# One hybrid decoder layer in fp32: the engines' queues ordered by the detailed timeline model instead of the simple one

## The chip, the cores and the metric

The kernel runs on one core of a Trainium2 chip. The metric is the device time of one launch in microseconds (us). The engines named here are PE (TensorE, matmuls; PEld is its weight load), DVE (VectorE), ACT (ScalarE), POOL (GpSimd) and SP (SyncE, which issues the DMAs). Each engine works through its own queue strictly in order, and waits at the head of it on semaphores that other engines or DMAs raise. [...]

## The reference

One decoder layer on 256 tokens of width 2048, batch 1, depth 1, all in fp32. A conditioning vector c gives shifts, scales and gates for both halves. Eight heads are stick-breaking attention, eight are sparse attention (DSA) over the 64 best keys of an indexer.

```
mod = silu(c) @ w_ada + b_ada
sh1, sc1, g1, sh2, sc2, g2 = split(mod, 6)
h = rmsnorm(x, norm1_g) * (1 + sc1) + sh1
q_sb, k_sb, v_sb, q_ds, k_ds, v_ds, q_ix, k_ix, w_ix = split(h @ w_in)
# stick-breaking: w[t,s] = exp(log_sigmoid(z[t,s]) + sum over s<j<t of log_sigmoid(-z[t,j])), s < t
o_sb = stick_breaking_attention(q_sb, k_sb, v_sb)       # z = q k^T / sqrt(128)
o_ds = dsa_attention(q_ds, k_ds, v_ds, q_ix, k_ix, w_ix) # top 64 keys of a score, softmax, p @ v
merged = concat(rmsnorm(o_sb, sb_norm_g), rmsnorm(o_ds, dsa_norm_g))
x = x + g1 * (merged @ w_out)
h2 = rmsnorm(x, norm2_g) * (1 + sc2) + sh2
u = causal_conv3(h2 @ w_up) ; gate, val = split(u)       # 2 x 5504 columns
x = x + g2 * ((silu(gate) * val) @ w_down)
return rmsnorm(x, final_norm_g)
```

## The kernel before

Everything lies transposed in the on-chip memory: features on the 128 partitions, tokens along the free axis. Each fp32 weight piece of 1 MB is loaded by SP, and each half of it is split into a high part (a cast on ACT, L145, names ending in h) and a low part (a subtraction on DVE, L146, names ending in l). A product is then three matmuls per 128 x 128 block: high by high, low by high and high by low (L173 to L175 in `trn`, which gives the transposed result). The raw pieces have 4 buffers, and so have the high and the low parts.

The stages in program order: the norm of x and the adaLN vector; the columns of `w_in` for the indexer and the DSA heads; the DSA heads with their norm (sums of squares rdsp, broadcast rdsb, reciprocal root rdsy at L126, normalised od split into odh and odl); the values V; then for each stick-breaking head h the projection QK(h) (chunks QK10 to QK17 in the names) and `sb_head(h)`; then the output projection O in groups of column blocks, the first half of it on the DSA heads (O<-odh, odl), the second half on the stick-breaking heads (O<-osh, osl), which needs their norm (rsbp, rsbv, rsby, rsbb); then the FFN with its up (U) and down (W) products.

A stick-breaking head goes back and forth between three engines:

```
z = pt[:, 0:384]                                   # L671-673: three matmuls on PE
A.copy(out=zs, in_=z)                              # L675
A.activation(e, z, AF.Abs)                         # L677, then Exp L678 and Ln L679
V.scalar_tensor_tensor(out=e, in0=z, scalar=0.0, in1=e, op0=ALU.max, op1=ALU.add)   # L680
T.matmul(pt[:, 0:384], lhsT=negu, rhs=e, start=True, stop=False)                    # u, L682-683
V.tensor_tensor(out=w, in0=pt[:, 0:384], in1=zs, op=ALU.add)                        # L685
A.activation(w, w, AF.Exp)                                                          # L686
T.matmul(po[:, 0:S], lhsT=vsb[:, 0, h * P:(h + 1) * P], rhs=w[:, 0:S], ...)         # o, L688-689
A.activation(os_[:, h, :], po[:, 0:S], AF.Copy, ...)                                # L690
A.activation(sq, po[:, 0:S], AF.Square)                                             # L695
V.tensor_tensor(out=sqs, in0=sqs, in1=sq, op=ALU.add)                               # L696
```

z, u and o, the DSA matmuls and the broadcasts of the norms share four PSUM banks (tag att), which are handed out in program order; QK, V and O share the other four (tag acc). So z of head 0 cannot stand ahead of rdsb in PE's queue.

Between the stages `pump()` issues pieces of the adaLN product for the later shifts and gates: most as a multiplication with a running sum on DVE (wa, L225), five groups as matmuls on PE (ap, L202, 4 loads wg of 4 matmuls each, transposed by aq, L210).

The program does not fix the order between independent instructions. When the context that L964 opens is closed, a scheduling pass plays the whole program through on a model of the engines, and at each step puts next into an engine's queue the earliest instruction in program order that is ready by the model's time. What stands in the queues is then fixed; on the chip each engine keeps to it.

## Time and profile before

| | |
|---|---|
| three runs | 1221.39 us median (1220.79 to 1223.54) |
| profiled execution | 1222.48 us, span 1220.7 us from the first to the last instruction |
| mean granted clock of TensorE | 0.976 |
| busy | PE 1154.4 us (95%), DVE 879.5 (72%), ACT 632.2 (52%) |
| DMA | 303.48 MB, mean 249 GB/s |
| the chain that ended last | PE 89%, DVE 6%, ACT 3%, DMA 1% |

The engine with the largest share is PE. The chain that ended last is followed back from the last instruction, at each step to what released it; PE's 89% of it says that for most of the span the next matmul waited only for the one before it.

### The profile page before, as it was taken

To read this page: it belongs to the slowest core of one execution; us is meant where nothing else is said; L and a number is where in the kernel's file an instruction comes from. 1 tells how busy PE (TensorE), PEld (TensorE's weight loads), DVE (VectorE), ACT (ScalarE), POOL (GpSimd) and SP (SyncE) were. 2 spreads that over 40 slices of the span, in tenths; PEclk is the share of its full clock that TensorE was granted. 3 is DMA by queue.
4 is the path that set the end of the run, shared out by engine and by line. 5 is a ranking of instruction groups with operands and counts; after the bars stand their busy time and mean duration, and the time that the engine had idled before them with its cause. 6 is when DMAs were issued, how large, how long until landed. Compare 5 with 4: busy or idle time off the path is not lost.

```text
span 1220.7 us, 17725 instructions
## 1 busy us (share of the span) xinstructions
PE 1154.4 (95%) x7120; PEld 1018.6 (83%) x7120; DVE 879.5 (72%) x1267; ACT 632.2 (52%) x1004; POOL 0.2 (0%) x4
## 2 busy tenths in 40 slices
PE   3699999899999797999999999999999999999996
PEld 2578997668878797999888888888888888888885
DVE  4877787689766698878789787787876745454543
ACT  3356554457465344456565556555655644444441
POOL 0000000000000000000000000000000000000000
PEclk9799999899999898999999999999999999999998
DMA  8988899668788498776568666675665555555541
GB/s 308 391 318 333 330 324 335 256 222 329 260 341 331 141 346 306 246 275 238 177 246 336 241 210 225 222 254 208 246 224 202 178 198 183 196 184 189 191 139 69
DMA packets 43282, 303.48 MB, mean 249 GB/s; under 512 B 4928, under 2 KB 5440, under 8 KB 7232
## 3 DMA queue, kind: packets, MB, share of 16 engines
q1 hardware_dynamic: 43200, 302.35, 68.1%
q8 instruction: 55, 0.90, 0.3%
q14 instruction: 27, 0.22, 0.0%
HBM read 300.24 MB, written 2.10 MB: 248 GB/s over the span
## 4 chain that ended last, share of the span: by engine, by line
PE 89%; DVE 6%; ACT 3%; DMA 1%; issue 1%; SPq 0%; DVEq 0%; ACTq 0%
PE U L168 21%; PE W L168 13%; PE U L166 11%; PE W L166 7%; PE U L173 3%; PE U L174 3%; PE U L175 3%; PE O L174 3%; PE O L175 3%; PE QK L173 3%; PE QK L175 3%; PE O L173 3%; PE QK L174 3%; DVE wa L225 2%; PE ap L202 1%; PE A L151 1%
## 5 line engine op out<-in xcount | busy, mean ns | idle before, releaser
L225 DVE SCALAR_TENSOR_TENSOR wa<-wa,scb 128x2048 f32<-128x2048 f32 x76 | 173.2, 2284 | 3.8 <-DMA wa<-wa 3.5
L844 ACT COPY u<-U 128x256 f32<-128x256 f32 x70 | 26.1, 372 | 116.6 <-PE U L168 116.6
L845 DVE TENSOR_TENSOR u<-U,u 128x256 f32<-128x256 f32 x70 | 29.3, 420 | 58.7 <-ACT u L844 58.7
L855 DVE SCALAR_TENSOR_TENSOR uc<-u,par,uc 128x255 f32<-128x255 f32 (+1 forms) x140 | 63.8, 478 | 0.8
L851 ACT ACTIVATE uc<-u,par 128x256 f32<-128x256 f32 x70 | 41.9, 601 | 0.0
L862 ACT CAST aT<-uc 128x256 fp32r<-128x256 f32 x43 | 17.4, 404 | 33.3 <-DVE uc L861 33.3
L323 ACT ACTIVATE amul<-mod,b,par 128x1 f32<-128x1 f32 x32 | 12.1, 385 | 42.8 <-DVE wa L225 42.6
L890 DVE SCALAR_TENSOR_TENSOR x1T<-W,mod,x1T 128x256 f32<-128x256 f32 x16 | 7.7, 481 | 31.1 <-PE W L166 31.1
L741 ACT ACTIVATE x2q<-x1T 128x256 f32<-128x256 f32 x15 | 6.3, 418 | 39.1 <-DVE x1T L736 39.0
L326 ACT ACTIVATE mod<-mod,par 128x1 f32<-128x1 f32 x32 | 8.5, 294 | 30.5 <-DVE wa L225 29.4
L202 PE MATMUL ap<-wg,csil 128*32 128x512 f32 x160 | 23.5, 642 | 0.7 <-DMA wg<-wg 0.5
L857 ACT ACTIVATE uc<-uc 128x256 f32<-128x256 f32 x43 | 17.9, 416 | 7.7 <-DVE uc L855 7.6
L861 DVE TENSOR_TENSOR uc<-uc 128x256 f32<-128x256 f32 x43 | 18.2, 422 | 2.8
L863 DVE TENSOR_TENSOR aT<-uc,aT 128x256 fp32r<-128x256 f32 x43 | 18.0, 418 | 0.8 <-ACT aT L862 0.7
L855 DVE SCALAR_TENSOR_TENSOR uc<-U,par,uc 128x255 f32<-128x255 f32 (+1 forms) x32 | 15.0, 478 | 1.0 <-ACT uc L851 0.6
L686 ACT ACTIVATE sbt<-sbt 128x384 f32<-128x384 f32 x8 | 4.2, 525 | 20.6 <-DVE sbt L685 20.6
L202 PEld LDWEIGHTS ap<-wg,csil 128*32 128x32 f32 x160 | 4.3, 115 | 9.4 <-issue 7.0
L736 DVE SCALAR_TENSOR_TENSOR x1T<-O,mod,xT 128x256 f32<-128x256 f32 x16 | 7.0, 479 | 6.7 <-PE O L175 6.7
L555 PE MATMUL rel<-ws,qixT 64*128 64x128 f32 (+1 forms) x64 | 9.8, 390 | 1.5 <-ACT rl L560 1.5
L207 ACT COPY rw<-ap 128x512 f32<-128x512 f32 x5 | 2.9, 581 | 15.5 <-PE ap L202 15.5
L283 PE MATMUL cb<-ident,csil 128*128 128x128 f32 x16 | 3.6, 423 | 7.6 <-DMA ident<-ident 7.6
L151 PE MATMUL A<-wA00h,hh 128*128 128x512 f32 x4 | 2.5, 669 | 8.5 <-ACT hh L318 8.5
(2810 smaller groups left out, 4042.8 us busy)
## 6 DMA issues: line engine op xcount, KB each, us to landing
wU<-wU SPq DMA_DIRECT2D x86, 1024.0 KB, 4.8
wa<-wa SPq DMA_DIRECT2D x76, 1024.0 KB, 6.3
wD<-wD SPq DMA_DIRECT2D x43, 1024.0 KB, 4.8
wg<-wg SPq DMA_DIRECT2D x20, 1024.0 KB, 7.1
wA<-wA SPq DMA_DIRECT2D x16, 1024.0 KB, 6.7
wQK<-wQK SPq DMA_DIRECT2D x16, 1024.0 KB, 6.1
wO<-wO SPq DMA_DIRECT2D x16, 1024.0 KB, 5.7
xT<-xT SPq DMA_DIRECT2D x4, 512.0 KB, 6.0
```

Source lines behind the costliest of these rows:

```text
L166: T.matmul(pt[:, 1, :], lhsT=wl, rhs=x[:, 0, :], start=False, stop=stop)
L168: T.matmul(pt, lhsT=wh, rhs=x, start=first, stop=stop)
L173: T.matmul(pt, lhsT=wh, rhs=xh, start=first, stop=False)
L174: T.matmul(pt, lhsT=wh, rhs=xl, start=False, stop=False)
L175: T.matmul(pt, lhsT=wl, rhs=xh, start=False, stop=last)
L202: T.matmul(pt[32 * j:32 * j + 32, :], lhsT=csil[:, k:k + 1].to_broadcast([P, 32]), rhs=w[:, j * 512:(j + 1) * 512], start=q == 0, stop=q == 3)
L225: i = V.scalar_tensor_tensor(out=w, in0=w, scalar=1.0, in1=scb, op0=ALU.mult, op1=ALU.mult, accum_out=mod[:, j:j + 1])
L844: A.copy(out=u[:, gv, :], in_=acc[gv][:, 1, :])
L845: V.tensor_tensor(out=u[:, gv, :], in0=acc[gv][:, 0, :], in1=u[:, gv, :], op=ALU.add)
L851: A.activation(uc[:, gv, :], u[:, gv, :], AF.Identity, scale=par[:, PCW + 3 * i + 2:PCW + 3 * i + 3], bias=par[:, PCB + i:PCB + i + 1])
L855: V.scalar_tensor_tensor(out=uc[:, gv, sft:S], in0=u[:, gv, 0:S - sft], scalar=par[:, o:o + 1], in1=uc[:, gv, sft:S], op0=ALU.mult, op1=AL ...
L861: V.tensor_tensor(out=uc[:, 1, :], in0=uc[:, 0, :], in1=uc[:, 1, :], op=ALU.mult)
```

## The change

The context is opened with the detailed timeline model for its scheduling pass:

```diff
-    with tile.TileContext(nc) as tc:
+    with tile.TileContext(nc, schedule_with_timeline_sim=True) as tc:
         layer(tc, aps, out)
```

No instruction is added or removed. PE's list of 4226 rows differs from the one before in 1418 lines; DVE's and ACT's differ with it. In SP's queue only three loads near the masks at the start change places, and POOL's is the same.

On PE, where the first stick-breaking head begins (z_2529 is its z), the order before is as follows; QK_2554 and QK_2647 are the projections QK11 and QK12, and rdsb is the broadcast of the DSA norm.

```order
L175 MATMUL QK_2554<-hh_1352,wQK1110l 128x256
L173 MATMUL QK_2647<-hh_1352,wQK1200h 128x256
L174 MATMUL QK_2647<-hl_1353,wQK1200h 128x256
L129 MATMUL rdsb<-ident,rdsy 128x128 x2
L671 LDWEIGHTS identb
L671 MATMUL z_2529<-sbm,identb 128x384
L672 MATMUL z_2529<-qk_198 128x256
L673 MATMUL z_2529<-qk_198 128x128
L175 MATMUL QK_2647<-hh_1352,wQK1200l 128x256
L173 MATMUL QK_2647<-hh_1352,wQK1200h 128x256
```

Behind it follow 284 more matmuls of QK12 to QK17, mixed with u0, o0, z1 and the next heads. After the change the same z stands here, with the last DSA steps (av, pp), the last adaLN product (ap_3184) and the sum rdsp in front of it, and a matmul of the first O block behind it:

```order
L637 MATMUL av_2248<-pT_2171,ws 128x512
L202 MATMUL ap_3184<-wg_3197,csil 32x512 x4
L637 MATMUL av_2256<-pT_2171,ws 128x512 x2
L202 MATMUL ap_3184<-wg_3266,csil 32x512 x4
L115 MATMUL rdsp<-nones,dsq 128x1 x4
L129 MATMUL rdsb<-ident,rdsy 128x128 x2
L671 LDWEIGHTS identb
L671 MATMUL z_2529<-sbm,identb 128x384
L672 MATMUL z_2529<-qk_198 128x256
L673 MATMUL z_2529<-qk_198 128x128
L173 MATMUL O_3204<-odh,wO000h 128x256
```

All 286 matmuls of QK12 to QK17 that stood behind z0, and 32 matmuls of the two adaLN groups ap52 and ap76 (16 each), now stand ahead of it, between steps of the DSA heads. Between z0 and z2 now stand the first halves of O0 and O1 and most of O2 and O3, 192 matmuls up to u2.

Further on in PE's queue, from u of head 2 (u_2724) to u of head 3 (u_2805), the order after the change is:

```order
L683 MATMUL u_2724<-sbt,nones 128x128
L688 MATMUL o_2729<-sbt,vsb 128x256
L689 MATMUL o_2729<-sbt,vsb 128x128
L671 LDWEIGHTS identb
L671 MATMUL z_2796<-sbm,identb 128x384
L672 MATMUL z_2796<-qk_198 128x256
L673 MATMUL z_2796<-qk_198 128x128
L682 MATMUL u_2805<-sbt,cst 128x384
L683 MATMUL u_2805<-sbt,nones 128x128
```

The same pattern goes on to o of head 7, and rsbp, rsbb and the second half of O0 follow; nothing stands between u and o of a head or between o and the next z. In the order before, QK matmuls, the adaLN groups and O0 to O3 stood between z, u and o of each of these heads, as here around z and u of head 5 (z_2990, u_2999):

```order
L671 MATMUL z_2990<-sbm,identb 128x384
L672 MATMUL z_2990<-qk_199 128x256
L673 MATMUL z_2990<-qk_199 128x128
L202 MATMUL ap_3184<-wg_3185,csil 32x512 x3
L202 MATMUL ap_3184<-wg_3191,csil 32x512 x4
L202 MATMUL ap_3184<-wg_3197,csil 32x512 x4
L682 MATMUL u_2999<-sbt,cst 128x384
```

On DVE, around the reciprocal root of the DSA norm (rdsy, L126), the order before is:

```order
L146 TENSOR_TENSOR wQK1200l<-wQK_2648,wQK1200h 128x1024
L121 TENSOR_SCALAR rdsv<-rdsp 128x2
L146 TENSOR_TENSOR wQK1210l<-wQK_2648,wQK1210h 128x1024
L124 SCALAR_TENSOR_TENSOR rdsl<-rdsy 128x2
L125 TENSOR_TENSOR rdsl<-rdsl,rdsv 128x2
L126 SCALAR_TENSOR_TENSOR rdsy<-rdsl,rdsy 128x2
L355 SCALAR_TENSOR_TENSOR qk_198<-QK_2554,qk_198 128x256
```

and after the change:

```order
L146 TENSOR_TENSOR wO100l<-wO_3280,wO100h 128x1024
L146 TENSOR_TENSOR wO101l<-wO_3280,wO101h 128x1024
L121 TENSOR_SCALAR rdsv<-rdsp 128x2
L124 SCALAR_TENSOR_TENSOR rdsl<-rdsy 128x2
L225 SCALAR_TENSOR_TENSOR wa_3338,mod<-wa_3338,scb 128x2048
L125 TENSOR_TENSOR rdsl<-rdsl,rdsv 128x2
L225 SCALAR_TENSOR_TENSOR wa_3341,mod<-wa_3341,scb 128x2048
L126 SCALAR_TENSOR_TENSOR rdsy<-rdsl,rdsy 128x2
```

Thirty-eight more instructions stand ahead of L126: 10 splits of wQK, 4 of wO, 8 reductions wa, 14 puts of QK into qk (L353, L355) and two small ones; none moved the other way. The reduction wa that stood between rsbv and rsby, the same steps of the later norm, no longer stands there. On ACT 21 instructions, mostly the casts that belong to those splits, moved ahead of the same place.

## Rows read from the trace of the kernel before

**Rows 1.** The page: busy time by engine, and the costliest group.

```profile
PE 1154.4 (95%) x7120; PEld 1018.6 (83%) x7120; DVE 879.5 (72%) x1267; ACT 632.2 (52%) x1004; POOL 0.2 (0%) x4
...
L225 DVE SCALAR_TENSOR_TENSOR wa<-wa,scb 128x2048 f32<-128x2048 f32 x76 | 173.2, 2284 | 3.8 <-DMA wa<-wa 3.5
```

**Rows 2.** Busy time by stage; columns as in its head line.

```profile
core 0: us, PE busy (x) PEld busy (x) DVE busy (x) ACT busy (x) POOL busy (x), PEclk, DMA share, GB/s
...
222.00:302.30 80.30, 74.88 (x435) 55.21 (x429) 69.46 (x176) 50.45 (x123) 0.00 (x0) 0.94 0.69 261
302.30:357.00 54.70, 54.13 (x394) 46.31 (x392) 40.62 (x55) 26.89 (x52) 0.00 (x0) 1.00 0.81 306
...
395.00:405.00 10.00, 2.01 (x7) 1.31 (x7) 8.03 (x11) 3.90 (x7) 0.00 (x0) 0.66 0.57 220
...
485.00:1205.00 720.00, 720.00 (x4366) 648.24 (x4366) 505.42 (x698) 383.09 (x547) 0.00 (x0) 1.00 0.60 213
```

**Rows 3.** Timeline of one head: start, duration, engine, line [idle before].

```profile
356.60 0.33 PE L671 MATMUL z<-sbm,identb 128*128 128x384 bf16 x1
...
357.50 2.77 PE L202 MATMUL ap<-wg,csil 128*32 128x512 f32 x22
357.57 0.43 DVE L696 TENSOR_TENSOR ws<-ws,sbt 128x256 f32<-128x256 f32 x1 [1.85 <-ACT sbt L695]
...
359.62 0.56 DVE L680 SCALAR_TENSOR_TENSOR sbt<-z,sbt 128x384 f32<-128x384 f32 x1 [1.62 <-ACT sbt L679]
...
360.24 0.91 PE L682 MATMUL u<-sbt,cst 128*128 128x384 f32 x2
...
361.41 0.56 DVE L685 TENSOR_TENSOR sbt<-u,sbt 128x384 f32<-128x384 f32 x1 [1.23 <-PE u L683]
361.88 1.22 DVE L146 TENSOR_TENSOR wO000l<-wO,wO000h 128x1024 fp32r<-128x1024 f32 x1
362.00 0.52 ACT L686 ACTIVATE sbt<-sbt 128x384 f32<-128x384 f32 x1 [0.53 <-DVE sbt L685]
...
363.38 0.59 PE L688 MATMUL o<-sbt,vsb 128*128 128x256 f32 x2
...
364.03 0.33 PE L671 MATMUL z<-sbm,identb 128*128 128x384 bf16 x1
```

**Rows 4.** The chain of waits, 408 to 409 us: start, duration, what.

```profile
408.05 0.21 PE O L174
...
408.64 0.12 PE O L174
```

**Rows 5.** Timeline at the first head's z.

```profile
302.30 0.33 PE L671 MATMUL z<-sbm,identb 128*128 128x384 bf16 x1
...
302.38 0.41 DVE L353 TENSOR_TENSOR qk<-QK,qk 128x256 f32<-128x256 f32 x1
```

**Rows 6.** Short windows with the granted clock (PEclk), columns as rows 2.

```profile
230.00:235.00 5.00, 3.48 (x30) 2.55 (x27) 4.15 (x10) 5.00 (x7) 0.00 (x0) 0.94 0.61 231
235.00:240.00 5.00, 5.00 (x15) 2.81 (x15) 5.00 (x16) 2.79 (x6) 0.00 (x0) 0.50 0.47 188
...
400.00:405.00 5.00, 1.74 (x6) 1.04 (x6) 4.13 (x4) 2.46 (x3) 0.00 (x0) 0.50 0.71 297
```

**Rows 7.** Timeline of the stick-breaking norm, 394 to 404 us.

```profile
394.50 0.50 PE L115 MATMUL rsbp<-nones,ws 128*128 128x1 f32 x4
...
396.86 0.15 DVE L121 TENSOR_SCALAR rsbv<-rsbp 128x2 f32<-128x2 f32 x1
396.93 2.28 DVE L225 SCALAR_TENSOR_TENSOR wa<-wa,scb 128x2048 f32<-128x2048 f32 x1
...
399.74 0.69 PE L129 MATMUL rsbb<-ident,rsby 128*128 128x128 f32 x2 [4.73 <-DVE rsby L126]
...
403.22 0.58 PE L173 MATMUL O<-osh,wO010h 128*128 128x256 f32 x1 [2.80 <-ACT osh L656]
```

**Rows 8.** Waits of PE, 215 to 410 us: total, times, longest.

```profile
PE rsbb L129 <- DVE rsby L126: 4.7, 1, 4.7
```

## The prediction

> **What bounds the kernel now.** I read the page first: TensorE (PE) is busy for 1154 us of 1220.7, 95% [rows 1]. So there are about 66 us in which PE stands still, and the kernel can only change in two ways: those 66 us grow or shrink, or the granted clock is lower for longer. Then I cut the span into stages [rows 2]. From 485 us to 1205 us PE is busy for 720.00 of 720 us at clock 1.00: the whole FFN is paced by PE, and whatever is late when it begins stays late to the end. VectorE (DVE) has 505 us of work there, so a split that stands a place or two further back in its queue still comes in time; I put that whole stretch, and the first 222 us, at 0, with 2 us either way in the range. What is left is 222 to 405 us: the end of the sparse (DSA) heads, the QK projections, the eight stick-breaking heads, the O projections and the norm in front of their second half. There the three stretches shown are idle on PE for 5.4, 0.6 and 8.0 us.
>
> The timeline of one stick-breaking head [rows 3] is the key. The reader is to see a strict chain across three engines: z on PE from 356.60, done by 357.50 when the next PE work starts; four ScalarE (ACT) steps and L680 on DVE; u on PE from 360.24; L685 on DVE at 361.41; the last exponential on ACT at 362.00, 0.52 long; then o on PE. From z to a ready o is 5.9 us, and o to the next head's z is 0.65 us (363.38 to 364.03), so a head alone needs 6.6 us. PE works in it for 0.9 + 1.15 + 0.65 = 2.7 us. In the kernel before, the other 3.9 us cost nothing, since matmuls of other stages stand in PE's queue there: 22 records of the adaLN product run between z and u of this head, and the three stretches show how little PE idles from 302 to 357 us although five heads are under way.
>
> **The change part by part.** No instruction is added or taken away; only places in queues change. In front of z0 PE now has all that it did behind it: 286 matmuls of the projections QK12 to QK17 and 32 of the adaLN product. At 0.12 us from one matmul to the next (the last of [rows 4]), the first are 34.3 us; the adaLN matmuls are two records each, so 22 records in 2.77 us [rows 3] make 0.25 us each and 8.0 us for 32. PE therefore reaches z0 42.3 us later than at 302.30 [rows 5], at 344.6, less what it fills. It can fill at most the 5.4 us of idle from 222 to 302, and win back about 5 us of half clock there (a mean clock of 0.94 over 80.3 us [rows 2] is 4.8 us lost; one such stretch is 235 to 240 us [rows 6]): 334 at the earliest. DVE gives a second bound: ahead of rdsy (L126), which releases the broadcast rdsb that stands right before z0, there are now 38 more instructions, 8 reductions wa at 2.28 us [rows 1], 14 splits at 1.22 us [rows 3] and 14 puts of QK at 0.41 us [rows 5], plus two tiny ones: 18.3 + 17.1 + 5.7 = 41.1 us. DVE was idle for 80.3 - 69.5 = 10.8 us in that stretch, so it is there between 332.6 and 343.4. Two bounds of nearly the same size leave z0 between 334 and 350 (the 344.6, and the 5.4 us of idle once more if the end of the DSA heads, with less other work between its steps, waits as long again). I take 341: most of the idle in that stretch is waiting inside the DSA chain itself, and that chain is still there, but some of it now has QK matmuls in it.
>
> From z0 to the end of the first half of O0 to O3 PE has 192 matmuls of O at 0.12, 23.0 us, two heads and z2, 2 x 2.7 + 0.9 = 6.3 us, and at the start the wait for the normalised od, for which the same chain took 3.5 us on the other norm (399.74 to 403.22) [rows 7]: together 33 us. So the O matmuls, which were the cover for heads 5 to 7 and for the time after them, are used up beside heads 0 and 1. **Behind them heads 2 to 7 stand bare**: in the new order there is nothing between u2, o2, z3, u3 and so on to o7. Head 2 ends with u, DVE, ACT and o: 1.15 + 0.6 + 0.5 + 0.65 = 2.9 us; then five heads at 6.6 us are 33 us. Of these PE idles for 5 x 3.9 = 19.5 us, where before it did useful work. This is where the loss comes from.
>
> Then the norm rsb. Behind the last o come three small steps (o of head 4 ended by 356.60, its sum L696 by 358.00: 1.4 us) [rows 3]. From rsbp at 394.50 to rsbv at 396.86 it took 2.36 us with a split of wO in the way; bounds are 0.5 (the sum's own time) and 2.4, I take 1.8. From rsbv to rsbb it took 2.88 us, of which 2.28 were a reduction wa that stood between; in the new order the four steps stand together, so 0.6. From rsbb to the first matmul of the second half 3.5 us. Together 7.3 us [rows 7]. That is a gain of 2.9 us on this norm, and the sum has it.
>
> The second half of O so begins at 341 + 33 + 2.9 + 33 + 7.3 = 417.2, against 403.22: **14.0 us later at full clock**. Next the clock. While PE sat in the gaps of the old norm it fell to 0.50 (400 to 405 us), and with PE busy for only 3.48 of the 5 us before, it was 0.50 from 235 to 240 as well [rows 6]; a matmul of O was 0.21 us apart then and 0.12 after [rows 4]. The bare heads leave PE working 2.7 of 6.6 us, less than in the 5 us ahead of that earlier fall. So I take 1.2 GHz from the second bare head on: PE's 2.7 us double, 4 x 2.7 = 10.8 us. Bounds: 0 if the clock stays up, 13.5 if all five heads have it. [...]
>
> Everything behind is paced by PE, so the delay is carried to the end: +24.8 us. The profiled execution took 1222.5 us; 1222.5 + 24.8 = 1247.3. It lies 1.1 us above the median of the three runs, so a median of 1246.
>
> **The rivals.** *Full clock in the bare heads.* Each has three stints of PE work in 6.6 us, and from 302 to 357 us with all gaps filled the clock was 1.00. Then only the 14.0 us are left: 1235. Against it speak the two falls named. *z0 later still.* If DVE's wa reductions wait for their loads and nothing of the idle is filled, z0 comes at 350, and all five bare heads run at half clock: 350 - 341 = 9, + 13.5, + 14.0 = 36.5 us: 1258. The longest wait on PE in this region was 4.7 us, for rsby behind such a wa [rows 8], which shows that the queue can do this; against it, DVE has idle time to catch up. *The other side: faster.* All depends on where z0 falls: the second half of O begins 76.2 us after it, so z0 by 403.2 - 76.2 = 327 at full clock breaks even. It would need the QK and wa work that now stands ahead to be taken up almost wholly by time that is now idle or half clocked between 222 and 302, that is 17.6 us of PE's 42.3 and 16.4 of DVE's 41.1. PE has 5.4 + 4.8 us there and DVE 10.8, so it fails by some 6 to 7 us on both engines; only if the bare heads were also shorter than 6.6 us could it win. With z0 at 320 the time would be 1214. *The order does not matter,* because the same work lies on PE: it would need a cover for the bare heads which the new order doesn't have.
>
> **How the numbers follow.** Half clock from the second bare head on, 1246: 0.60. Full clock, 1235: 0.17. Later z0, 1258: 0.13. Faster, 1214: 0.06. No change: 0.04. The range: from 1229 (z0 at 334 and full clock: +7 us) to 1262 (the late case with 2 us more from the stretches at both sides and 2 from the norm), with about 0.15 left out. A measurement of this kernel tells some 0.2% (2.4 us) from no change. Faster 0.06, same 0.04, slower 0.90.
>
> **What would show it.** In the changed kernel's profile z0 should stand at 334 to 350 us; PE should be gapless or nearly so for some 30 us behind it; then heads of 6.6 us (9.3 at 1.2 GHz) each from head 3 on, with PE busy about 40% and waits on sbt from L680 and L686; the granted clock at 0.5 in that stretch; the reduction wa gone from the wait for rsby; the FFN as before in length, only moved. I am wrong if z0 comes before 327, if matmuls of other stages are found between u and o of heads 3 to 7, or if the FFN's length differs by more than 2 us.

## The result and the profile after

The changed kernel takes 1270.3 us (median of 4 runs, 1270.08 to 1272.05) against 1221.09 us for the kernel before beside it: ratio 1.0403, 95% interval 1.0385 to 1.0421. It is 49 us slower; the forecast was 25 us slower, 1246 us, with a range that ended at 1262.

The page of the changed kernel: busy time by engine.

```profile
span 1269.5 us, 17757 instructions
...
PE 1173.3 (92%) x7120; PEld 1030.4 (81%) x7120; DVE 881.7 (69%) x1267; ACT 630.3 (50%) x1004; POOL 0.2 (0%) x4
```

The same 7120 matmul records as in [rows 1] are busy for 18.9 us longer, and PE stands still for 1269.5 - 1173.3 = 96.2 us instead of 1220.7 - 1154.4 = 66.3. Both parts of the loss are there: 30 us of idle, and 19 us of slower matmuls (mean granted clock, as a share of the full clock, 0.959, before 0.976).

Busy time by stage; the first window ends at z of head 0, the second at z of head 3, the third at the norm rsbp, the fourth at the second half of O.

```profile
core 0: us, PE busy (x) PEld busy (x) DVE busy (x) ACT busy (x) POOL busy (x), PEclk, DMA share, GB/s
222.00:361.38 139.38, 123.15 (x789) 92.53 (x789) 109.53 (x221) 67.27 (x145) 0.00 (x0) 0.96 0.86 321
361.38:399.60 38.22, 34.82 (x237) 32.88 (x236) 22.36 (x24) 20.71 (x36) 0.00 (x0) 0.88 0.52 198
399.60:443.70 44.10, 23.38 (x67) 16.56 (x65) 8.13 (x16) 16.68 (x37) 0.00 (x0) 0.64 0.05 20
443.70:449.40 5.70, 1.64 (x6) 1.19 (x6) 2.99 (x7) 1.88 (x4) 0.00 (x0) 0.50 0.01 3
```

z0 stands at 361.4 us, where [rows 5] had 302.3: 59.1 us later, not 38.7. The bare heads are in the third window: PE busy for 23.4 of 44.1 us at a mean clock of 0.64. The second half of O begins at 449.41 against 403.22 [rows 7], 46.2 us later, and the FFN 48.8 us later (533.14 against 484.38); the rest of the span is the same length.

The waits of PE from 222 us to z0, then from 360 to 450 us: total, times, longest.

```profile
PE rdsb L129 <- DVE rdsy L126: 5.5, 1, 5.5
PE qdsp L598 <- DVE qds L306: 4.2, 1, 4.2
PE rdsp L115 <- DVE dsq L645: 3.1, 1, 3.1
...
PE u L682 <- DVE sbt L680: 13.6, 6, 2.7
PE o L688 <- ACT sbt L686: 8.0, 6, 2.0
...
PE rsbb L129 <- DVE rsby L126: 1.3, 1, 1.3
```

Of the 16.2 us that PE stands still ahead of z0 (139.38 - 123.15), the first three waits are 12.8, and none of the three is among PE's waits in the same stretch before. In each PE waits for a step of the DSA chain on DVE.

The wait of rsbb, 4.7 us in [rows 8], is down to 1.3 with the reduction wa gone, as forecast. Its twin at the DSA norm, rdsb, now has 5.5, because two reductions stand between the steps that lead to rdsy:

```profile
356.04 0.16 DVE L124 SCALAR_TENSOR_TENSOR rdsl<-rdsy 128x2 f32<-128x2 f32 x1
356.12 2.29 DVE L225 SCALAR_TENSOR_TENSOR wa<-wa,scb 128x2048 f32<-128x2048 f32 x1
...
358.34 0.15 DVE L125 TENSOR_TENSOR rdsl<-rdsl,rdsv 128x2 f32<-128x2 f32 x1
358.41 2.28 DVE L225 SCALAR_TENSOR_TENSOR wa<-wa,scb 128x2048 f32<-128x2048 f32 x1
...
360.62 0.16 DVE L126 SCALAR_TENSOR_TENSOR rdsy<-rdsl,rdsy 128x2 f32<-128x2 f32 x1
```

The timeline of a bare head, to be read against [rows 3]:

```profile
407.01 0.53 PE L671 MATMUL z<-sbm,identb 128*128 128x384 bf16 x1
...
410.86 0.56 DVE L680 SCALAR_TENSOR_TENSOR sbt<-z,sbt 128x384 f32<-128x384 f32 x1 [2.41 <-ACT sbt L679]
...
411.48 1.65 PE L682 MATMUL u<-sbt,cst 128*128 128x384 f32 x2 [2.66 <-DVE sbt L680]
...
414.76 1.22 PE L688 MATMUL o<-sbt,vsb 128*128 128x256 f32 x2 [1.20 <-ACT sbt L686]
...
416.20 0.53 PE L671 MATMUL z<-sbm,identb 128*128 128x384 bf16 x1
```

It takes 9.2 us from z to z, with 2.66 + 1.20 us of idle on PE, and each matmul is longer than in [rows 3] (u 1.65 us instead of 0.91). The idle is the same in all five bare heads; the granted clock is not. Three of them, heads 4 to 6, one to a row:

```profile
407.00:416.20 9.20, 5.33 (x15) 3.71 (x13) 1.54 (x3) 3.19 (x7) 0.00 (x0) 0.50 0.00 1
416.20:424.40 8.20, 4.33 (x14) 3.21 (x13) 1.54 (x3) 3.19 (x7) 0.00 (x0) 0.71 0.00 0
424.40:433.60 9.20, 5.33 (x15) 3.71 (x13) 1.54 (x3) 3.19 (x7) 0.00 (x0) 0.50 0.00 0
```

Heads 4 and 6 are at half clock (0.50) throughout; in windows of 1 us, head 5 between them shows 0.50 up to 418 us, 1.00 from 419 to 421 and 0.50 again from 422 on, and it is 1 us shorter.

Much of why z0 is so late is seen on DVE, in a chain that ends 60 us ahead of it. The indexer picks its 64 keys by eight rounds of MAX8 (L578) and MATCH_REPLACE8 (L579) for each half of the tokens, each round on the result of the one before. All 16 MAX8 of both kernels, before and then after (duration min/median/max in ns, first and last start):

```profile
L578 DVE MAX8 m<-scw x16: 280/344/417, 239.6 to 258.4; 128x8 f32<-128x128 f32 x8, 128x8 f32<-128x256 f32 x8
```

```profile
L578 DVE MAX8 m<-scw x16: 285/352/428, 243.9 to 300.7; 128x8 f32<-128x128 f32 x8, 128x8 f32<-128x256 f32 x8
```

Each MAX8 is as long as before within 3%; from the first start to the last the chain takes 56.8 us instead of 18.8. One round of it after the change, from one MAX8 to the next, takes 7.5 us:

```profile
275.41 0.42 DVE L578 MAX8 m<-scw 128x8 f32<-128x256 f32 x1
275.75 2.27 DVE L225 SCALAR_TENSOR_TENSOR wa<-wa,scb 128x2048 f32<-128x2048 f32 x1
...
277.95 1.22 DVE L146 TENSOR_TENSOR wQK1100l<-wQK,wQK1100h 128x1024 fp32r<-128x1024 f32 x1
...
279.16 0.41 DVE L579 MATCH_REPLACE8 scw<-m,scw 128x256 f32<-128x256 f32 x1
279.49 2.28 DVE L225 SCALAR_TENSOR_TENSOR wa<-wa,scb 128x2048 f32<-128x2048 f32 x1
...
282.89 0.42 DVE L578 MAX8 m<-scw 128x8 f32<-128x256 f32 x1
```

Here a reduction and a split stand between a MAX8 and its MATCH_REPLACE8, and a reduction behind it. From the first MAX8 to the last, eight reductions (wa32 to wa39) and ten splits are in the chain, against no reduction and one split before; together they are busy for 30.5 us (before 1.2). DVE is idle there for 5.5 us, 3.1 of them ahead of a split that waits for its cast on ACT (before: not idle). The first softmax exponential follows at 301.8 us (before 265.3), and by the first transpose behind it PE has used up QK10 to QK13 and most of QK14.

### The profile page after: what moved, and what is told of

Its sections match the earlier page's. It is cut to its first block, busy times and chain, and to the rows that moved or that the text cites. A ratio compares the mean times of both kernels' runs of the same rounds, so it can differ in the third digit from the quotient of the medians.

```text
span 1269.5 us, 17757 instructions
## 1 busy us (share of the span) xinstructions
PE 1173.3 (92%) x7120; PEld 1030.4 (81%) x7120; DVE 881.7 (69%) x1267; ACT 630.3 (50%) x1004; POOL 0.2 (0%) x4
## 4 chain that ended last, share of the span: by engine, by line
PE 78%; DVE 9%; DMA 7%; ACT 3%; issue 2%; SPq 0%; DVEq 0%; ACTq 0%
PE U L168 20%; PE W L168 12%; PE U L166 11%; PE W L166 6%; DMA wa<-wa 4%; DVE wa L225 4%; PE O L174 3%; PE O L173 3%; PE O L175 3%; PE U L174 2%; PE U L175 2%; PE U L173 2%; PE ap L202 1%; PE V L152 1%; PE QK L175 1%
## 5 line engine op out<-in xcount | busy, mean ns | idle before, releaser
L855 DVE SCALAR_TENSOR_TENSOR uc<-u,par,uc 128x255 f32<-128x255 f32 (+1 forms) x140 | 66.5, 478 | 2.4 <-ACT uc L851 1.8
L857 ACT ACTIVATE uc<-uc 128x256 f32<-128x256 f32 x43 | 17.7, 412 | 14.4 <-DVE uc L855 14.4
L682 PE MATMUL u<-sbt,cst 128*128 128x384 f32 x16 | 8.5, 621 | 13.6 <-DVE sbt L680 13.6
L326 ACT ACTIVATE mod<-mod,par 128x1 f32<-128x1 f32 x32 | 8.4, 290 | 24.3 <-DVE wa L225 22.0
L688 PE MATMUL o<-sbt,vsb 128*128 128x256 f32 x16 | 8.0, 595 | 8.0 <-ACT sbt L686 8.0
L696 DVE TENSOR_TENSOR ws<-ws,sbt 128x256 f32<-128x256 f32 x7 | 3.0, 426 | 17.7 <-ACT sbt L695 17.7
L682 PEld LDWEIGHTS u<-sbt,cst 128*128 128x128 f32 x16 | 2.8, 219 | 15.1 <-DVE sbt L680 14.7
L680 DVE SCALAR_TENSOR_TENSOR sbt<-z,sbt 128x384 f32<-128x384 f32 x8 | 4.4, 556 | 12.4 <-ACT sbt L679 12.4
```

Of the source, the lines that this page charges most:

```text
L855: V.scalar_tensor_tensor(out=uc[:, gv, sft:S], in0=u[:, gv, 0:S - sft], scalar=par[:, o:o + 1], in1=uc[:, gv, sft:S], op0=ALU.mult, op1=AL ...
```

## The experiments

Ratios are to the kernel before, run beside each (medians 1219 to 1222 us). "z0" is the first L671, "O" the first matmul of the second half of O; the changed kernel has 361.4 and 449.4, the kernel before 302.3 and 403.2. `order(a, b)` puts a behind b in the queue of their engine and adds no wait for b's result. The edits are given in short, with plain names for the handles; they add lines, so the line numbers in a run's rows lie some lines behind those of the kernel before.

**1. QK12 to QK17 held back behind rdsb**, in the changed kernel:

```diff
+                    if pi == last_p and h >= 2:
+                        order(first_matmul, rdsb)
```

> The changed kernel, with one thing put back: every matmul of the projections QK12 to QK17 is queued behind the broadcast rdsb, so that z0 stands ahead of them on PE as it did before. Theory A (the loss is that this work is spent before the heads, on a DSA chain that did not need it): z0 comes at 313 to 319 us instead of 361, heads 0 to 5 are covered again, only heads 6 and 7 stand bare; second half of O near 417 us, total near 1237 us (1228 to 1245). Rival B (the loss comes from other places of the new order, such as the splits and reductions on DVE or the FFN's order): z0 may move, but the total stays above 1255.

1272.0 us, ratio 1.0426 (1.0407 to 1.0445): no gain at all, and the total is where rival B had it. z0 came at 336.1, not at 313 to 319, and O at 450.5. PE was busy for 97.2 of the 114.4 us between them, so the heads were mostly covered; but the DSA chain was hardly earlier (first exponential 299.0), and what had covered it was gone. Waits of PE, 285 to 336 us:

```profile
PE pp L637 <- ACT p L632: 16.9, 4, 12.6
PE av L643 <- ACT pT L638: 2.9, 2, 1.6
```

So the place of QK in PE's queue is not the cause by itself: while the DSA chain is late, PE idles either in the heads or ahead of them. The idle only moved.

**2. The first halves of O0 to O3 dealt out to the heads**, in the changed kernel:

```diff
+                if s == 0 and m < 4:
+                    order(first_matmul_of_half, z[2 * m + p_])
```

> The changed kernel, with the first halves of O0 to O3 dealt out to the heads: each block of 24 matmuls is queued behind z of one head, eight blocks for eight heads. z0 stays at 361 us. Theory A (bare heads on PE, and the half clock that they bring, cost what lies between z0 and the second half of O): 8 heads at 6.6 us and the norm make 64 us instead of 88, so the total falls by some 24 us to 1246 (1241 to 1252). Rival C (the heads' own chain over ACT and DVE is the limit however PE is filled, 8 to 9 us a head): total 1262 to 1270.

1258.6 us, 1.0320 (1.0298 to 1.0341): 12 us back, half of what theory A gave. z0 to O fell from 88.0 to 74.8 us, heads behind the first at 6.7 to 9.5 us: between the two theories, and inside neither's range. In several heads a split of wO now stands on DVE between u and L685, and PE waits 2.4 us for o instead of 1.2:

```profile
408.30 0.38 PE L687 MATMUL u<-sbt,nones 128*128 128x128 f32 x2
408.75 1.23 DVE L150 TENSOR_TENSOR wO011l<-wO,wO011h 128x1024 fp32r<-128x1024 f32 x1 [1.26 <-ACT wO011h L149]
409.90 0.55 DVE L689 TENSOR_TENSOR sbt<-u,sbt 128x384 f32<-128x384 f32 x1
...
411.06 0.70 PE L692 MATMUL o<-sbt,vsb 128*128 128x256 f32 x2 [2.38 <-ACT sbt L690]
```

**3. All heads behind all of QK, in the kernel before:**

```diff
         do_QK(last_p, h)
         pump()
+    for h in range(NH):
         sb_head(h)
         pump()
```

> The kernel before, simple model, with all eight heads written behind all of QK10 to QK17 in the program. z0 comes behind QK17, some 35 us later than before, but the DSA chain is still mixed with V and QK10 to QK12, and O0 to O2 with the adaLN matmuls are dealt out between the heads. Theory A (a late z0 costs only what stands bare on PE): heads at 6.6 us, nothing bare but the norm: 1222 us (1217 to 1228). Rival D (the lateness of z0 itself costs, as the prediction's sum from z0 had it): 1236 to 1258.

1226.6 us, 1.0057 (1.0040 to 1.0074). z0 at 336.4, 34 us later, and O only 4.4 us later. PE is busy for 109.1 of the 114.4 us from 222 us to z0 and 56.6 of the 71.2 behind it. A late z0 is not itself a loss; what counts is whether PE has work on the way. Rival D falls.

**4. Six casts of wQK on ACT behind the first exponentials**, in the changed kernel:

```diff
+                if pi == last_p and 2 <= h <= 4:
+                    order(cast, last_exp_of_first_half)
```

> The changed kernel, with the six casts of wQK12 to wQK14 on ACT queued behind the first softmax exponentials of the DSA heads instead of ahead of them; the rest of the order follows from the model. Theory A1 (z0 is late because those casts wait for their loads with the softmax behind them): first exponential near 280 us instead of 302, z0 near 340 instead of 361; 11 us of QK16 and QK17 and adaLN work then lie behind z0, so the second half of O gains 8 to 14 us and the total is near 1260 (1255 to 1264). Rival E (the DSA chain is late by PE's queue or by DVE whatever ACT does): first exponential earlier, z0 still later than 352, total above 1266.

1266.5 us, 1.0380 (1.0359 to 1.0400). Neither theory fits: the total lies at the edge of rival E and z0, at 344.9, near theory A1's 340. But the first exponential came at 293.2, not 280, and O only 4.7 us earlier, with 69 matmuls of QK16 and QK17 moved behind z0. ACT then waited 12.1 us for nm, the maximum that the softmax needs, on DVE, where it stands behind the last MAX8. The casts held the softmax for 8.6 us at most; what holds the rest is the selection chain, as experiment 5 shows.

**5. The selection chain freed**, in the changed kernel: wa32 to wa39 and the splits of wQK behind its end.

```diff
+        if 32 <= j < 40:
+            order(wa, end_of_selection)
...
+                if pi == last_p:
+                    order(split_on_DVE, end_of_selection)
```

> The changed kernel, with the eight reductions wa32 to wa39 and the splits of wQK on DVE queued behind the end of the top-k selection (16 MAX8 steps in a chain), instead of between its steps. Theory F (z0 is late because the selection's serial steps wait in DVE's queue for those 18 instructions): the selection ends near 263 us instead of 301, the first exponential is near 269 instead of 302, z0 near 337 to 345 instead of 361; heads 3 to 7 still stand bare, so z0 to the second half of O stays 90 to 95 us: total near 1252 (1246 to 1258). Rival A1 (the casts on ACT hold the softmax): first exponential stays above 290 and the total above 1262.

1259.7 us, 1.0316 (1.0300 to 1.0333).

```profile
L586 DVE MAX8 m<-scw x16: 281/351/428, 243.0 to 267.3; 128x8 f32<-128x128 f32 x8, 128x8 f32<-128x256 f32 x8
```

The last MAX8 starts at 267.3, the first exponential at 269.6, z0 at 342.7: theory F's stations, within 5 us. The time missed its range by 2 us: z0 moved by 18.6 us, O by 10.6. 32 matmuls of QK17 and the 16 of ap76, some 8 us, now stand behind z0, and heads 3 to 7 are still bare (z0 to O 96 us). Up to z0:

```profile
222.00:342.74 120.74, 113.08 (x724) 88.14 (x717) 98.28 (x206) 61.17 (x137) 0.00 (x0) 0.97 0.75 288
```

PE is idle for 7.7 us there instead of 16.2. The two reductions ahead of rdsy are still where they were, but PE has matmuls of QK16 and QK17 to run meanwhile, and its wait for rdsy is gone.

**6. Only the splits kept out of the selection:**

```diff
+                if pi == last_p:
+                    order(split_on_DVE, end_of_selection)
```

> As the run before, but the splits of wQK alone are queued behind the selection; the reductions wa stay between its steps. Theory F: seven reductions at 2.3 us stay in the chain, so it ends near 279 us, the first exponential is near 285, z0 near 345 to 352, total near 1258 (1252 to 1264). Rival F2 (the splits, which wait for casts and loads, make nearly all of the delay): the selection ends below 270 and the total is within 3 us of the run before.

1263.4 us, 1.0352 (1.0337 to 1.0367).

```profile
L584 DVE MAX8 m<-scw x16: 284/352/428, 243.2 to 284.9; 128x8 f32<-128x128 f32 x8, 128x8 f32<-128x256 f32 x8
```

The first exponential came at 285.9, as theory F had it, and the total is in its range; the chain is 41.7 us long. Between 56.8 us with both and 24.3 with neither, splits make 15.1 us of the delay and reductions 17.4, about half each; F2 falls. (z0 at 339.7 is earlier than theory F's 345 and no later than in experiment 5, since 76 more matmuls of QK15 to QK17, 9 us, stand behind it.)

**7. Selection freed, wa65 and wa66 behind rdsy, and O dealt out**, the edits of 2, 5 and 9 together:

> The changed kernel with both causes taken away by order alone: nothing between the selection's steps, wa65 and wa66 behind rdsy, and O0 to O3 dealt out so that each block of 24 matmuls of O stands behind one head's z. Theories F and A together (late DSA chain and bare heads are the whole loss): z0 near 337, heads at 7 to 8 us, second half of O near 411, total 1230 (1222 to 1238). Rival G (something else of the new order costs as well): total above 1243.

1248.4 us, 1.0230 (1.0215 to 1.0244): above the theories' range and inside rival G's. z0 came near what was expected (343.3), but O at 427.9 instead of 411. PE was busy for 62.1 of the 84.6 us between. The heads took 8 to 12 us: O dealt out by halves is a weak cover, as in experiment 2. So this run can't tell G from a weak cover; experiments 10 and 11 use a stronger one.

**8. PE kept busy in the bare heads by matmuls that do nothing.** The changed kernel; in heads 3 to 7 ten matmuls on constants ahead of u and four ahead of o, written to unused columns; z, u and o stay in the same order. It adds work whose results nothing reads.

```diff
+        for _ in range(10 if h >= 3 else 0):
+            T.matmul(pt[:, 384:512], lhsT=ident, rhs=ident, start=True, stop=True)
```

> The changed kernel with work added: in the bare heads 3 to 7, ten matmuls of 128 columns on constants stand between z and u and four between u and o, in unused columns of the banks of u and o; their results are read by nobody. Nothing else is moved. Theory K (half clock doubles PE's part of a bare head): with PE kept busy the clock stays at 1.00, a head takes 6.6 to 7 us instead of 8.3 on average, the five heads 33 to 35 us instead of 41.7, the norm behind them starts at full clock, total 1258 to 1263. Rival L (ACT and DVE set a bare head's length and the clock hardly matters): heads stay above 8 us, total 1268 or more.

1260.3 us, 1.0326 (1.0310 to 1.0341): 10 us faster than the changed kernel with 70 matmuls more. The same 42 us of both, changed kernel and then this one:

```profile
400.00:442.00 42.00, 22.66 (x64) 16.14 (x62) 7.70 (x15) 15.72 (x35) 0.00 (x0) 0.64 0.04 19
```

```profile
400.00:442.00 42.00, 32.38 (x214) 27.88 (x214) 13.34 (x24) 18.77 (x40) 0.00 (x0) 0.95 0.03 12
```

The clock goes from 0.64 to 0.95, and the time from z of head 3 to o of head 7 from 41.7 to 33.2 us, 6.7 us from z to z instead of 8.5. ACT and DVE do the same work in both, so rival L falls and theory K holds: some 8.5 us of the loss in the heads is half clock. Heads 4 to 6 of the changed kernel are at 0.50, 0.71 and 0.50 with idles of 2.66 and 1.20 us in each; with the added matmuls PE waits for only 0.43 us ahead of u and 0.31 ahead of o of head 4. What makes the clock go up and down in the changed kernel is not shown by any run.

**9. wa65 and wa66 behind rdsy**, in the changed kernel:

```diff
+        if j in (65, 66):
+            order(wa, rdsy)
```

> The changed kernel, with the two reductions wa65 and wa66 queued behind rdsy (L126) instead of between the steps that lead to it. Theory: the wait of rdsb for rdsy falls from 5.5 to about 1 us, z0 comes 4.4 us earlier, near 357, and the total falls by 4 to 6 us to 1265. Rival: the 4.6 us come back behind z0, where the two reductions then stand in the way of L654 and L680: total within 2 us of the changed kernel.

1267.2 us, 1.0385 (1.0364 to 1.0405). z0 came 5.5 us earlier (355.9), O 4.0 us, the total 3 us, which the two intervals do not tell from nothing. Of the 5.5 us, 2.0 were there already at the first exponential (299.8), ahead of the place of the edit. The waits of PE from 340 to 372 us:

```profile
PE O L177 <- ACT odh L662: 2.1, 1, 2.1
PE rdsb L131 <- DVE rdsy L128: 1.8, 1, 1.8
PE O L178 <- DVE odl L663: 1.8, 1, 1.8
```

The wait for rdsy fell from 5.5 to 1.8 us, 3.7 us less. The waits for the normalised od, 1.2 us in the changed kernel, are now 3.9, because one reduction stands in front of the product od (L654) and the other behind it. So most of it was given back, as the rival had it.

**10. The heads two deep**, in the changed kernel: z of head h + 1 is written ahead of u and o of head h.

```diff
-        sb_head(h)
+        nxt = sb_head(h)              # z up to L680
+        if h:
+            sb_tail(h - 1, *prev)     # from u on
+        prev = nxt
```

> The changed kernel, with the heads written two deep: the z stage of head h+1 stands in the program ahead of the u and o stages of head h. z0 stays near 361. Theory A (the serial chain of a head on PE, ACT and DVE is what costs behind z0): two heads in flight make a bare head 4 to 5 us instead of 8.3, z0 to the second half of O falls from 88 to 62 to 70 us, total 1245 to 1253. Rival M (ACT, with seven steps a head, or DVE is full in this stretch): less than 8 us gained, total above 1262.

1240.7 us, 1.0167 (1.0150 to 1.0184): 30 us back, more than expected, and the largest gain of any single edit. z0 stayed at 360.6, O came at 418.8; the last heads follow each other by some 4 us. The timeline of one of them:

```profile
400.57 0.33 PE L671 MATMUL z<-sbm,identb 128*128 128x384 bf16 x1
...
401.39 0.81 PE L685 MATMUL u<-sbt,cst 128*128 128x384 f32 x2
...
403.62 0.70 PE L691 MATMUL o<-sbt,vsb 128*128 128x256 f32 x2 [1.21 <-ACT sbt L689]
...
404.38 0.33 PE L671 MATMUL z<-sbm,identb 128*128 128x384 bf16 x1
```

u of one head starts right behind z of the next, with no wait in front of it; only o still waits. Theory A holds for the part behind z0, and rival M falls.

**11. Both causes undone by the means that worked**: the edits of 5, 9 and 10 together, in the changed kernel.

> The changed kernel with both causes taken away at once: nothing of wa32 to wa39 or of the splits of wQK between the selection's steps, wa65 and wa66 behind rdsy, and the heads written two deep. Theories F and A together are the whole loss: z0 near 342, z0 to the second half of O 60 to 66 us, so that half begins near 405, total 1222 to 1230, most of the 49 us back. Rival G (something else of the new order costs as well): total above 1235.

1230.2 us, 1.0068 (1.0051 to 1.0084): 40 of the 49 us are back, at the very edge of what the two theories gave, and rival G's 1235 is not reached. z0 342.1, O 408.2, FFN at 492.1. From 222 us to z0 and from z0 to O:

```profile
222.00:342.09 120.09, 112.25 (x727) 86.84 (x726) 98.81 (x207) 61.24 (x137) 0.00 (x0) 0.99 0.75 293
342.09:408.18 66.09, 54.33 (x373) 46.16 (x370) 45.02 (x62) 42.47 (x85) 0.00 (x0) 0.95 0.70 271
```

Against experiment 10 the edits of 5 and 9 together bring O forward by 10.6 us, as much as 5 did alone. Of the 7.7 us by which the FFN is still late, 5.0 are there when O begins, and 2.2 come from the FFN's first matmul, which waits 4.9 us for h (before 2.7). These 2.2 us are the changed kernel's too; nothing was tried on them.

**12 and 13. The kernel before, improved.** First, the norm of the stick-breaking heads is written ahead of O2 instead of behind O3 (the new lines in short; the old ones behind O3 are taken out):

```diff
     for m in range(4):
+        if m == 2:
+            rms_b([sqs], NH * HD, rsb, "rsb", "att")
+            norm_o(os_, rsb, osh, osl)
         do_O(acc[m], m, 0, odh, odl)
```

> The kernel before, simple model; the norm of the stick-breaking heads and its products are written ahead of O2 in the program instead of behind O3, so that rsbp and rsbb stand between matmuls of O2 in PE's queue and O2 and O3 cover the norm. Theory H (PE idle at 395 to 405 us, 8.0 us, and the half clock behind it are pure loss): 9 to 13 us faster than before, near 1209. Rival I (DVE and ACT, which also split wO, delay O2 and O3 by as much): 0 to 4 us faster.

1210.2 us, 0.9916 (0.9902 to 0.9930), 10 us faster than the kernel before: theory H. Where [rows 2] had 2.01 us of PE work in 10 us, nothing is idle now:

```profile
376.00:392.00 16.00, 16.00 (x135) 15.95 (x134) 14.02 (x18) 9.31 (x17) 0.00 (x0) 1.00 0.75 281
392.00:402.00 10.00, 10.00 (x85) 10.00 (x84) 8.34 (x10) 5.10 (x7) 0.00 (x0) 1.00 0.89 328
```

Then the heads two deep besides, as in experiment 10:

> The kernel before, simple model, with the early norm of the run that beat it and the heads two deep. Theory A: the heads were covered already, so two deep changes little: 1206 to 1213, within 4 us of the early norm alone. Rival N (two heads in flight keep more of ACT and DVE from the splits, and QK and O wait for them): above 1214.

1209.2 us, 0.9907 (0.9892 to 0.9922): the same within the intervals. Where the heads are covered, their chain costs nothing that these runs can tell. So the 30 us of experiment 10 are the price of bare heads, and not a gain that any order would have. Both versions beat both kernels.

## Why the prediction was wrong

**The direction and its reason held.** Heads 3 to 7 stand bare, PE idles in each of them for 2.66 and 1.20 us (3.9 was the forecast), and the granted clock, 0.64 in the mean, is 0.50 in 31 of the 44 windows of 1 us from 400 to 444 us, 1.00 in 8 and between the two in 5; experiments 8 and 10 show both causes. A head wholly at half clock takes 9.2 us, for which the prediction had 9.3. No run shows the 1.2 GHz that the prediction takes for these heads, or any clock in GHz; what the runs show in its place is a granted clock of 0.50 in heads 4 and 6, where PE is busy for 5.33 us of a head (2 x 2.7 = 5.4 in the sum). That the clock would fall in the bare heads was the author's estimate from the falls in [rows 6]; why it falls, no run shows. The stretch from z0 to O was put at 76.2 + 10.8 = 87.0 us and measured 88.0. That this is so close is in part luck: up to z of head 3 it had 35.9 us against 38.2, for the five heads to rsbp 45.2 against 44.1, and for the rest of the norm 5.9 against 5.7.

**The step that failed is the time of z0**: "Two bounds of nearly the same size leave z0 between 334 and 350". It came at 361.4, 20.4 us behind the 341 of the sum, and that is most of the 24 us that the sum lacked; 1.0 us lies between z0 and O, 2.6 us behind O. The work that the bounds moved was nearly right: on DVE 41.1 us, where the rows show 109.5 us busy up to z0 against 69.5, 40.0 more; on PE 42.3, where they show 123.2 against 74.9, 48.3 more, so 6 us too few. What was wrong is the other half of each bound, that the idle time is filled or, at worst, stays as it was: 350 is the whole of the work and the old 5.4 us once more. DVE's idle went from 10.8 to 139.4 - 109.5 = 29.9 us and PE's from 5.4 to 16.2, where the 341 leave PE 341 - 222 = 119 us for 74.9 + 42.3 of work, 1.8 of idle. These 14.4 us of idle and the 6 us of work are the 20.4.

**What stands in its place.** A bound made of sums asks how much work stands ahead of z0 and not between which steps of a chain it stands. The 18 reductions and splits in the selection, 30.5 us, lie between steps that depend on each other, and they stand there instead of beside it. So everything behind the selection (softmax, transposes, products, norm) began 37 us late; by the first transpose PE had used up QK10 to QK13 and most of QK14, and 8.6 of PE's 16.2 us of idle lie in its two last waits ahead of z0, for dsq and for rdsy, when no QK matmul was left. Experiment 5 shows it: with the selection free, z0 comes at 342.7, with some 8 us of work moved behind it, and PE's idle ahead of it is 7.7 us. At O that is worth 10.6 us of the 21.4 by which the sum missed it there. The other half is not shown by an edit of its own.

In the changed kernel z0's time counts because the work from z0 to O stays the same; experiment 4, where work moves along with z0, loses 4.4 us at O by a z0 that is 34 us late.

**The rival "z0 later still" had the right sign and too little of it**: it let DVE's reductions wait for their loads and put z0 at the upper bound of 350, 9 us later; z0 lies 11 us beyond that bound. One such wait is there: DVE stands still for 5.8 us in front of a reduction at 318.85. The profile puts it down to a matmul, but more likely it is the load, since the last loads of wa ahead of it were issued from 311.20 on, and such loads took 7.6 us to land (median from 305 to 325 us). It cost PE little, which was busy for 19.2 of the 20 us from 310 to 330; what PE waited for are steps of the DSA chain in DVE's queue. The two reductions ahead of rdsy stood in the order that is shown; they were summed and not priced as a wait. In the changed kernel that wait is 5.5 us; experiment 9 takes 3.7 of them away and gets about 3 us of the total at most.

**Smaller points.** The saving on the later norm came (rsbb waits 1.3 us instead of 4.7). The FFN kept its length, except for the 2.2 us at its start. In front of 222 us the change cost 0.2 us (the adaLN matmuls around 222 us end at 223.96 instead of 223.77), inside the 2 us allowed.

**What stays open.** Why the detailed model puts other work between the selection's steps wasn't measured: only the order that it made and the times on the chip are shown. And of the 49 us, experiment 11 gives back 40; of the rest, 5.0 us ahead of O and 2.2 us at the start of the FFN have no experiment of their own.

## What to carry to other kernels

When a change moves instructions, first follow each serial chain through the new queues, and price what stands between its steps; a sum of the work ahead of a point gives a lower bound only. In a kernel bound by one engine, the work that can cover a chain is a stock: used beside one chain, it is missing beside the next, and holding it back only moved the hole here (experiment 1); what helped was to shorten one chain (experiment 5) and to run the other two deep (experiment 10). A chain that ends in a norm or a broadcast wants its place in the program ahead of the last independent work, as in experiment 12.

## What was unexpected of the hardware

Added work made the kernel faster: 70 matmuls that nothing reads, in gaps of 2.66 and 1.20 us, took the granted clock of that stretch from 0.64 to 0.95 and the total down by 10 us. Without them the clock went up and down from head to head, 0.50, 0.71, 0.50, though the heads have the same work and the same gaps. And DVE's serial selection grew threefold, from 18.8 to 56.8 us, and hardly by slower instructions: the 16 MAX8 stayed at 0.35 us each. DVE was busy for 51.3 of the 56.8 us, 30.5 of them with the reductions and splits that the order put between.
